# The seam between out_proj and the up projection: weight buffers of the second and third pair exchanged, GpSimd's low parts and weight sums earlier, the last norm ahead of part of the operand sums

## The chip, the cores and the metric

One core of a Trainium2 chip runs the whole program, a decoder layer in fp32. The metric is the device time of one execution in microseconds, taken as the median of three runs. The engines are named as in the profile: PE is the matrix engine (TensorE), DVE is VectorE, ACT is ScalarE, POOL is GpSimd, and SP is the engine that issues most of the DMAs. Times are microseconds from the start of the span unless marked otherwise.

## The reference, cut to what matters

The layer has a mixing part (recurrence, attention and cross-attention, merged by gates) and a convolutional feed-forward part. The change lies where the first ends and the second begins:

```python
x = x + merged @ w_out[l]                 # out_proj
x = x + conv_ffn(x, norm2_g[l], w_up[l], conv_w[l], conv_b[l], w_down[l])

def conv_ffn(x, g, w_up, conv_w, conv_b, w_down):
    h = rms_norm(x, g) @ w_up             # 1024 x 1024 by 1024 x 5632
    acc = conv_b + hp[:, 0:t] * conv_w[0] + hp[:, 1:t+1] * conv_w[1] + hp[:, 2:t+2] * conv_w[2]
    gate, val = jnp.split(acc, 2, axis=-1)
    return (jax.nn.silu(gate) * val) @ w_down
```

Here `hp` is `h` with two rows of zeros ahead. The sequence and the model width are 1024, and `w_up` gives 2 x 2816 columns.

## The kernel before, in words

**Precision.** PE multiplies in fp32r. Each fp32 operand is split into a high part (ACT copies it to fp32r) and a low part (the operand minus the high part, on DVE or POOL). A product is three matmuls: high by high, high by low, low by high. So every operand of PE costs one ACT row and one DVE or POOL row before PE can use it.

**Out_proj and its norms.** `mm` multiplies a block of 128 tokens (tt = 0 to 7) by `w_out`. `norm(tt)` is a generator with two stops: it adds the residual to the two halves (L1346, DVE) and squares them with sums (ACT); it forms the reciprocal root (L1350, L179, and a small step of POOL on L180); then ACT scales the row (L1353). `spread(tt)` turns the scaled block over with eight transposes on PE (L105) and writes them into the operands `raw0`, `raw1` (L1368 on ACT, L1370 on DVE). The first seven blocks are done inside out_proj. Block 7 is left to the up projection: `up_phase` receives its norm as a generator and its spread as a function.

**The up projection.** `up_phase` works on 22 pairs of 128-column blocks of `w_up`. A pair is a 2 x 2 block product done with seven products instead of eight. Each product has 12 matmuls of 512 columns. Its operands on the token side are the blocks "11", "21", "22" and the sums T1 to T4; on the weight side they are the pair's raw blocks `w1`, `w2` and the sums of them. The token sums are the subtractions of `sums` (L1377); half 0 of it makes T1 and T2, half 1 the two others. `old` is tokens 0 to 383 of each half of the tokens, `new` is tokens 384 to 511, which only exist once block 7 is through its norm. `split_hi` (L1390, ACT) and `split_lo` (L1395, DVE, or POOL for "22") split the token operands.

**Weights of a pair.** `load(n)` fetches them (L1478). `prep1` splits `w1`. `prep2` forms two sums on POOL (`it`, L1504 and L1505) and splits them (L1482 on ACT, L1485 on POOL). `prep3` forms two differences on POOL (L1517 writes `w2`, L1518 writes `s4`) and splits them. Even pairs lie in the buffers `rw`, odd ones in `wr`. Pair 0's weights, and the first block of pair 1, are split earlier, in out_proj (`self.early`). The two buffers of `wr` hold the token sums t2 until the last `sums` and splits of T2 are through.

**Steps.** `step(n, i)` issues product i of pair n and the DVE or ACT rows that read its bank: step 6 adds p1 to the bank (L1607), and product 7 then goes on in the same bank, so PE waits for that DVE row; step 7 forms the second output `v` from the bank and from C (L1616, L1617), and product 3 goes on in bank C after that; step 4 subtracts D (L1626); step 3 closes the first output (L1633). `conv` applies the convolution: a start value on ACT (g, L1551), two DVE rows per half (L1552, L1553), then the gate (L1556, L1557 or L1562). `act_sums` forms four sums of the gated values for the down projection (L1570, gall) and sends them out.

**What sets the order.** A scheduler orders each engine's rows, except where a row is pinned: `self.pinned` and `keep_in_program_order` hold a row to its place in the program on its engine. PE's matmuls, the token operands and the first pairs' rows are pinned. On all engines but PE a row that waits holds the rows behind it.

The order around the seam is written out by hand in `up_phase` (from L1649 on), up to the loop over the pairs.

## Time and profile before

| | us |
|---|---|
| median of three runs | 1789.2 (1789.01, 1789.2, 1790.83) |
| the profiled execution | 1789.81 |
| its span | 1788.0 |

The span is the time between the first and the last instruction of the profiled execution. The rest of its time lies around it. The granted PE clock is 0.999 in the mean over the span.

A row of a timeline gives the start, the duration, the engine, the line, the operation, the output and inputs by their names, the shape and how many instructions it groups; a bracket gives the idle time of the engine just before and what ended it. For PE the same bracket is a wait of the matmuls themselves. In a view of waits, a row gives the waiting engine and line, what it waited for, and the total, the number of times and the longest. A row of the windows view gives the stretch, its length, the busy time and the number of rows of each engine, the granted clock as a share of full speed, the busy share of the DMA engines and GB/s. This is the chain of the page's fourth part, followed back from the last instruction, by engine:

```profile
PE 84%; DVE 4%; POOL 2%; ACT 1%; DMA 1%; issue 1%; DVEq 0%; SPq 0%; POOLq 0%; ACTq 0%
```

Most of the chain is PE. The costliest groups of the page are these (busy and mean of one instruction, then the idle time of the engine ahead of them and what ended most of it):

```profile
L119 PE MATMUL mm<-BT,l 128*128 128x512 f32 x504 | 117.9, 389 | 1.4 <-POOL l L1485 1.4
L119 PE MATMUL mm<-BT,wh 128*128 128x512 f32 x352 | 108.7, 389 | 0.9 <-DVE BT L1395 0.9
L1485 POOL TENSOR_TENSOR l<-it,l 128x1024 fp32r<-128x1024 f32 x21 | 50.8, 2419 | 90.2 <-ACT l L1482 90.2
```

The 504 matmuls that read the split weight sums waited 1.4 us in all, once; POOL, which makes the low parts, waited 90.2 us for ACT's high parts, which cost nothing as long as PE had other work.

### The profile page before, as it was taken

To read this page: it belongs to the slowest core of one execution; us is meant where nothing else is said; L and a number is where in the kernel's file an instruction comes from. 1 tells how busy PE (TensorE), PEld (TensorE's weight loads), DVE (VectorE), ACT (ScalarE), POOL (GpSimd) and SP (SyncE) were. 2 spreads that over 40 slices of the span, in tenths; PEclk is the share of its full clock that TensorE was granted. 3 is DMA by queue.
4 is the path that set the end of the run, shared out by engine and by line. 5 is a ranking of instruction groups with operands and counts; after the bars stand their busy time and mean duration, and the time that the engine had idled before them with its cause. 6 is when DMAs were issued, how large, how long until landed. Compare 5 with 4: busy or idle time off the path is not lost.

```text
span 1788.0 us, 27326 instructions
## 1 busy us (share of the span) xinstructions
PE 1774.1 (99%) x10479; PEld 1443.4 (81%) x10479; DVE 1178.8 (66%) x1604; ACT 863.6 (48%) x1566; POOL 794.3 (44%) x448
## 2 busy tenths in 40 slices
PE   9999999999999999999999999999999999999999
PEld 6777778888888888777777888877888888888887
DVE  5667774898988624234444962687767777795596
ACT  6544343556666635534444334544444445454443
POOL 3223352332331453122332542487777677545454
PEclk9999999999999999999999999999999999999999
DMA  5155565111112343567654553223323323396476
GB/s 210 59 162 180 183 224 159 51 54 57 54 57 77 125 120 96 207 227 278 208 190 177 197 191 108 104 95 106 112 89 98 121 89 122 126 321 216 146 239 208
DMA packets 122771, 261.28 MB, mean 146 GB/s; under 512 B 28681, under 2 KB 43657, under 8 KB 122514
## 3 DMA queue, kind: packets, MB, share of 16 engines
q1 hardware_dynamic: 85026, 193.83, 32.9%
q10 hardware_dynamic: 33840, 53.10, 8.1%
q0 software_dynamic: 3776, 12.62, 2.3%
q8 instruction: 82, 1.34, 0.3%
q14 instruction: 47, 0.39, 0.1%
HBM read 178.99 MB, written 80.48 MB: 145 GB/s over the span
## 4 chain that ended last, share of the span: by engine, by line
PE 84%; DVE 4%; POOL 2%; ACT 1%; DMA 1%; issue 1%; DVEq 0%; SPq 0%; POOLq 0%; ACTq 0%
PE mm L119 68%; PE g L119 12%; PE g L105 4%; DMA A<-yd 1%; POOL wl L1485 0%; DVE gall L1570 0%; DVE it L554 0%; DMA ggd<-qk 0%; DVE inst L556 0%; DVE qk L472 0%; POOL l L1485 0%; DVE w L832 0%; DMA x<-in_x_dram 0%; POOL it L1505 0%; DVE at L520 0%
## 5 line engine op out<-in xcount | busy, mean ns | idle before, releaser
L81 POOL TENSOR_TENSOR wl<-wr,wh 128x1024 fp32r<-128x1024 f32 (+2 forms) x78 | 199.2, 2554 | 469.6 <-ACT wh L80 469.6
L119 PE MATMUL mm<-xhi,wh 128*128 128x512 f32 x784 | 260.1, 412 | 1.0 <-ACT xhi L207 0.4
L119 PE MATMUL mm<-xlo,wh 128*128 128x512 f32 x784 | 243.4, 392 | 0.0
L119 PE MATMUL mm<-xhi,wl 128*128 128x512 f32 x784 | 242.5, 391 | 0.2 <-POOL wl L81 0.2
L119 PEld LDWEIGHTS mm<-xlo,wh 128*128 128x128 f32 x784 | 147.2, 188 | 33.1
L119 PEld LDWEIGHTS mm<-xhi,wl 128*128 128x128 f32 x784 | 146.9, 188 | 33.3 <-POOL wl L81 1.0
L119 PEld LDWEIGHTS mm<-xhi,wh 128*128 128x128 f32 x784 | 136.5, 189 | 29.3 <-issue 6.1
L80 ACT ACTIVATE wh<-wr 128x1024 fp32r<-128x1024 f32 (+2 forms) x78 | 81.8, 1049 | 131.1 <-PE mm L119 100.0
L119 PE MATMUL mm<-dw,da 128*128 128x512 f32 x528 | 120.3, 389 | 0.0
L119 PE MATMUL mm<-BT,l 128*128 128x512 f32 x504 | 117.9, 389 | 1.4 <-POOL l L1485 1.4
L1774 POOL TENSOR_TENSOR dw<-draw,dw 128x512 fp32r<-128x512 f32 x55 | 82.4, 1506 | 76.0 <-ACT dw L1772 72.2
L119 PEld LDWEIGHTS mm<-dw,da 128*128 128x128 f32 x528 | 99.1, 188 | 20.6
L119 PEld LDWEIGHTS mm<-BT,l 128*128 128x128 f32 x504 | 94.5, 188 | 21.4 <-POOL l L1485 1.8
L119 PE MATMUL mm<-BT,wh 128*128 128x512 f32 x352 | 108.7, 389 | 0.9 <-DVE BT L1395 0.9
L937 DVE TENSOR_TENSOR_SCAN at<-at,nrt 128x128 f32<-128x128 f32 (+3 forms) x64 | 96.4, 1514 | 19.5 <-ACT at L931 19.3
L119 PE MATMUL mm<-B,wh 128*128 128x512 f32 x352 | 108.5, 389 | 0.0
L1773 DVE TENSOR_TENSOR da<-draw,da 128x512 fp32r<-128x512 f32 x77 | 64.7, 846 | 51.3 <-ACT da L1771 49.4
L1485 POOL TENSOR_TENSOR l<-it,l 128x1024 fp32r<-128x1024 f32 x21 | 50.8, 2419 | 90.2 <-ACT l L1482 90.2
L119 PE MATMUL g<-dw,da 128*128 128x512 f32 x396 | 90.2, 389 | 0.0
L119 PEld LDWEIGHTS g<-dw,da 128*128 128x128 f32 x396 | 74.3, 188 | 15.4
L1771 ACT ACTIVATE da<-draw 128x512 fp32r<-128x512 f32 x77 | 48.1, 627 | 79.4 <-PE mm L119 32.2
L832 DVE TENSOR_TENSOR w<-w,nrt 128x1024 f32<-128x1024 f32 x24 | 46.6, 1940 | 57.3 <-ACT w L831 49.5
(337 smaller groups left out, 3980.3 us busy)
## 6 DMA issues: line engine op xcount, KB each, us to landing
wr<-in_w_in_dram SPq DMA_DIRECT2D x48, 512.0 KB, 3.6
draw<-actd SPq DMA_DIRECT2D x77, 256.0 KB, 3.4
draw<-in_w_down_dram SPq DMA_DIRECT2D x55, 256.0 KB, 4.4
at<-scr SPq DMA_DIRECT2D x24, 512.0 KB, 5.9
wr<-in_w_up_dram SPq DMA_DIRECT2D x22, 512.0 KB, 3.5
actd<-gall ACTq DMA_DIRECT2D x44, 256.0 KB, 3.0
rw<-in_w_up_dram SPq DMA_DIRECT2D x20, 512.0 KB, 3.6
gsd<-w ACTq DMA_DIRECT2D x18, 512.0 KB, 3.0
```

What stands on the lines that cost most here:

```text
L80: (fix_hi or fix)(self.nc.scalar.activation(hi, raw, AF.Copy))
L81: fix(self.nc.gpsimd.tensor_tensor(lo, raw, hi.bitcast(F32), ALU.subtract))
L105: self.pinned(self.nc.tensor.transpose(out, in_, self.ident[:n, :n]))
L119: self.pinned(self.nc.tensor.matmul(*a, **k))
L832: fix(nc.vector.tensor_tensor(g, g, self.nrb, ALU.mult))
L937: self.pinned(nc.vector.tensor_tensor_scan(sn[:, :W][:, ::-1], sn[:, :W][:, ::-1], self.nrt[:, 1152 - W :][:, ::-1], 1.0, ALU.mult, ALU.max))
L1485: ins = nc.gpsimd.tensor_tensor(lo, src, hi.bitcast(F32), ALU.subtract)
L1771: self.pinned(nc.scalar.activation(A[:, 0], a, AF.Copy))
L1773: self.pinned(nc.vector.tensor_tensor(A[:, 1], a, A[:, 0].bitcast(F32), ALU.subtract))
L1774: nc.gpsimd.tensor_tensor(Wt[:, 1], w, Wt[:, 0].bitcast(F32), ALU.subtract)
```

## The change

**Buffers.** `load` puts pairs 0, 2, 4 and so on into `wr` and the odd ones into `rw`. Pair 1's weights so no longer need t2's buffers, and are asked for (pinned on SP) right after the first stop of norm 7; the x of block 7 is asked for ahead of them, where it stood between the two loads of pair 2 before. Pair 2's weights now need t2's buffers.

**POOL.** The two sums of pair 1's weights become a function of their own (`weight_sums`) that is called right behind the norm's reciprocal root. The low parts of "22" stand ahead of that root. For pairs 1 and 2 the rows of `prep2` and `prep3` are pinned on POOL.

**DVE.** Half 1 of `sums(256, 384)` leaves out_proj. Its two parts (j = 0, 1) stand behind norm 7's residual adds, one ahead of the reciprocal root and one behind it. The last act_sums of pair 1 are split in two: two rows in step 6 of pair 2, two behind step 7's rows.

**ACT.** T2's second high part stands behind the norm's scaling; T1's second high part is done in one piece. T3's parts are split j by j, and pair 0's last weights are split ahead of T3's high parts.

The first of three places is POOL at the seam. Before (B is the low part of "22", `ss` the norm's small step, `it` the sums of pair 1's weights, `wl<-wsec` and `l<-wsum` low parts of pair 0's weights, `l<-it` that of pair 1's sums):

```order
L81 TENSOR_TENSOR wl_10501<-qk_10498,wh_10500 128x1024
L180 TENSOR_TENSOR ss_1592_10534<-rs_10542,half 128x1
L1395 TENSOR_TENSOR B_1_0_10511<-A_9821,B_0_0_10509 128x2x384
L1395 TENSOR_TENSOR B_1_1_10512<-A_9822,B_0_1_10510 128x2x384
L1485 TENSOR_TENSOR wl_10648<-wsec_10307,wh_10647 128x1024
L1395 TENSOR_TENSOR B_1_0_10511<-A_9821,B_0_0_10509 128x2x128
L1395 TENSOR_TENSOR B_1_1_10512<-A_9822,B_0_1_10510 128x2x128
L1504 TENSOR_TENSOR it_10690<-wr_10612 128x512
L1505 TENSOR_TENSOR it_10690<-it_10690,wr_10611 128x512
L1485 TENSOR_TENSOR l_1607_10674<-wsum_10308,l_1606_10673 128x512
L1485 TENSOR_TENSOR l_1611_10694<-it_10690,l_1610_10693 128x1024
```

and of the change:

```order
L81 TENSOR_TENSOR wl_10497<-qk_10494,wh_10496 128x1024
L1395 TENSOR_TENSOR B_1_0_10507<-A_9821,B_0_0_10505 128x2x384
L1395 TENSOR_TENSOR B_1_1_10508<-A_9822,B_0_1_10506 128x2x384
L180 TENSOR_TENSOR ss_1592_10528<-rs_10544,half 128x1
L1502 TENSOR_TENSOR it_10547<-rw_10535 128x512
L1503 TENSOR_TENSOR it_10547<-it_10547,rw_10534 128x512
L1487 TENSOR_TENSOR wl_10633<-wsec_10307,wh_10632 128x1024
```

The two low parts have moved ahead of the norm's step, and pair 1's sums follow it at once, where they stood behind four other rows.

The second place is DVE around norm 7's adds (`raw`, `A` and `t` are the token operands and sums, `x` the residual, `ss` and `rs` the norm, BT the low parts of T1 and T2). Before:

```order
L1377 TENSOR_TENSOR t_1522_9824<-A_9822,raw_9818 128x2x128
L1377 TENSOR_TENSOR A_9819<-A_9821,A_9819 128x2x128
L1377 TENSOR_TENSOR raw_9818<-t_1521_9823,raw_9818 128x2x128
L1377 TENSOR_TENSOR A_9820<-A_9822,A_9820 128x2x128
L1377 TENSOR_TENSOR raw_9818<-t_1522_9824,raw_9818 128x2x128
L1346 TENSOR_TENSOR x_1591_10531<-mm_10422,x_1591_10531 128x512
L1346 TENSOR_TENSOR x_1591_10531<-mm_10423,x_1591_10531 128x512
L1395 TENSOR_TENSOR BT_1_0_10515<-raw_9818,BT_0_0_10513 128x2x384
L1350 TENSOR_TENSOR ss_1592_10534<-ss_1592_10534 128x1
L179 TENSOR_SCALAR rs_10542<-ss_1592_10534 128x1
```

and of the change:

```order
L1377 TENSOR_TENSOR t_1522_9824<-A_9822,raw_9818 128x2x128
L1346 TENSOR_TENSOR x_1591_10525<-mm_10422,x_1591_10525 128x512
L1346 TENSOR_TENSOR x_1591_10525<-mm_10423,x_1591_10525 128x512
L1377 TENSOR_TENSOR A_9819<-A_9821,A_9819 128x2x128
L1377 TENSOR_TENSOR raw_9818<-t_1521_9823,raw_9818 128x2x128
L1350 TENSOR_TENSOR ss_1592_10528<-ss_1592_10528 128x1
L179 TENSOR_SCALAR rs_10544<-ss_1592_10528 128x1
L1377 TENSOR_TENSOR A_9820<-A_9822,A_9820 128x2x128
L1377 TENSOR_TENSOR raw_9818<-t_1522_9824,raw_9818 128x2x128
L1395 TENSOR_TENSOR BT_1_0_10511<-raw_9818,BT_0_0_10509 128x2x384
```

Four sums have moved behind the adds, two of them behind the reciprocal root, and T1's low part follows them.

The third place is POOL at pair 2's weights (`it` are their sums, L1517 and L1518, or L1522 and L1523, the differences, `l<-it` the low part of the sums, the second `wl` the low part of the differences). Before:

```order
L1485 TENSOR_TENSOR wl_10795<-rw_10762,wh_10794 128x1024
L1504 TENSOR_TENSOR it_10860<-rw_10763 128x512
L1505 TENSOR_TENSOR it_10860<-it_10860,rw_10762 128x512
L1517 TENSOR_TENSOR rw_10763<-rw_10762,rw_10763 128x512
L1518 TENSOR_TENSOR s_1646_10916<-rw_10762,it_10860 128x512
L1485 TENSOR_TENSOR l_1639_10864<-it_10860,l_1638_10863 128x1024
L1485 TENSOR_TENSOR wl_10920<-rw_10763,wh_10919 128x1024
```

and of the change:

```order
L1487 TENSOR_TENSOR wl_10794<-wr_10761,wh_10793 128x1024
L1502 TENSOR_TENSOR it_10859<-wr_10762 128x512
L1503 TENSOR_TENSOR it_10859<-it_10859,wr_10761 128x512
L1487 TENSOR_TENSOR l_1639_10863<-it_10859,l_1638_10862 128x1024
L1522 TENSOR_TENSOR wr_10762<-wr_10761,wr_10762 128x512
L1523 TENSOR_TENSOR s_1646_10915<-wr_10761,it_10859 128x512
```

The low part of the sums has moved ahead of the two differences. ACT's rows there keep their order: the high part of the sums, the high part of the differences (wh), and then the start values g of pair 1's convolution.

The diff:

```diff
--- before.py
+++ after.py
@@ -1372,11 +1372,11 @@
         def halves(j):
             return [raw0[:, 2 * j : 2 * j + 2], raw0[:, 4 + 2 * j : 6 + 2 * j], raw1[j], raw1[2 + j]]
 
-        def sums(t0, t1, which=(0, 1)):
+        def sums(t0, t1, which=(0, 1), js=(0, 1)):
             ts = slice(t0, t1)
             sub = lambda o, x, y: self.pinned(nc.vector.tensor_tensor(o, x, y, ALU.subtract))
             for half in which:
-                for j in range(2):
+                for j in js:
                     b11, b21, b12, b22 = (x[:, :, ts] for x in halves(j))
                     if half == 0:
                         sub(b11, b12, b11)
@@ -1410,7 +1410,7 @@
             elif tt == 5:
                 sums(0, 256)
             elif tt == 6:
-                sums(256, 384)
+                sums(256, 384, (0,))
 
         self.B, sqs = {}, {}
         t2 = [self.pool_wt.tile([128, 2, 512], F32, name=self.nm("t2"), tag="wr", bufs=2) for _ in range(2)]
@@ -1471,11 +1471,13 @@
 
         def load(n):
             if n < len(pairs):
-                tag, m = ("rw", pairs[n][0]) if n % 2 == 0 else ("wr", pairs[n][0])
-                pool = self.pool_r if n % 2 == 0 else self.pool_wt
+                tag, m = ("wr", pairs[n][0]) if n % 2 == 0 else ("rw", pairs[n][0])
+                pool = self.pool_wt if n % 2 == 0 else self.pool_r
                 W[n] = [pool.tile([128, 1024], F32, name=self.nm(tag), tag=tag, bufs=2) for _ in range(2)]
                 for i in range(2):
-                    nc.sync.dma_start(W[n][i], self.I["w_up"][m + i])
+                    ins = nc.sync.dma_start(W[n][i], self.I["w_up"][m + i])
+                    if n == 1:
+                        self.pinned(ins)
 
         def hl(src, pool, tags, n=1024, keep=False, queue=False):
             hi, lo = (pool.tile([128, n], F32R, name=self.nm(t), tag=t, bufs=16 if t == "l4" else 2) for t in tags)
@@ -1493,17 +1495,20 @@
             w = self.early[4 * n] if n < 2 else hl(W[n][0], self.pool_wt, ("wh", "wl"), keep=n == 2, queue=n == 2)
             st[n, 1], st[n, 2] = [[x[:, c] for x in w] for c in (L, R)]
 
+        def weight_sums(n):
+            w1, w2 = W[n]
+            s = st[n, "s"] = self.t4("it")
+            fix = self.tc.keep_in_program_order if n < 3 else lambda ins: ins
+            fix(nc.gpsimd.tensor_tensor(s[:, L], w2[:, L], w2[:, R], ALU.add))
+            fix(nc.gpsimd.tensor_tensor(s[:, R], s[:, L], w1[:, L], ALU.subtract))
+
         def prep2(n):
             if n == 0:
                 w = self.early[1]
             else:
-                w1, w2 = W[n]
-                s = self.t4("it")
-                st[n, "s"] = s
-                fix = self.tc.keep_in_program_order if n == 2 else lambda ins: ins
-                fix(nc.gpsimd.tensor_tensor(s[:, L], w2[:, L], w2[:, R], ALU.add))
-                fix(nc.gpsimd.tensor_tensor(s[:, R], s[:, L], w1[:, L], ALU.subtract))
-                w = hl(s, self.pool_l, ("l4", "l4"))
+                if n > 1:
+                    weight_sums(n)
+                w = hl(st[n, "s"], self.pool_l, ("l4", "l4"), keep=n == 1, queue=n < 3)
             st[n, 5], st[n, 6] = [[x[:, c] for x in w] for c in (L, R)]
 
         def prep3(n):
@@ -1513,10 +1518,10 @@
                 w1, w2 = W.pop(n)
                 s = st.pop((n, "s"))
                 s4 = self.pool_r.tile([128, 512], F32, name=self.nm("s4"), tag="s4", bufs=1)
-                fix = self.tc.keep_in_program_order if n == 1 else lambda ins: ins
+                fix = self.tc.keep_in_program_order if n < 3 else lambda ins: ins
                 fix(nc.gpsimd.tensor_tensor(w2[:, L], w1[:, L], w2[:, L], ALU.subtract))
                 fix(nc.gpsimd.tensor_tensor(s4, w1[:, R], s[:, R], ALU.subtract))
-            w = hl(w2, self.pool_wt, ("wh", "wl"), keep=n == 1, queue=n == 1)
+            w = hl(w2, self.pool_wt, ("wh", "wl"), keep=n < 2, queue=n < 2)
             st[n, 7], st[n, 4] = [[x[:, c] for x in w] for c in (L, R)]
             if n == 1:
                 return s4
@@ -1606,15 +1611,16 @@
                     st[n, "u1"] = u_tile()
                 self.pinned(nc.vector.tensor_tensor(st[n, "u1"][:, R2], Bk, st[n, "p1"], ALU.add))
                 if n and pairs[n - 1][2]:
-                    if n == 2:
-                        act_sums(pairs[n - 1][1], False)
-                    act_sums(pairs[n - 1][1], True)
+                    act_sums(pairs[n - 1][1], n > 2)
             elif i == 7:
                 Bk = st.pop((n, "B"))
                 product(n, 7, Bk, False, True)
                 v = st[n, "u2"] = u_tile()
                 nc.vector.tensor_tensor(v[:, L2], Bk, st.pop((n, "p1")), ALU.add)
-                nc.vector.tensor_tensor(v[:, R2], st[n, "C"], v[:, L2], ALU.add)
+                ins = nc.vector.tensor_tensor(v[:, R2], st[n, "C"], v[:, L2], ALU.add)
+                if n == 2:
+                    self.pinned(ins)
+                    act_sums(pairs[n - 1][1], True)
             elif i == 40:
                 Dk = st[n, "D"] = bank()
                 product(n, 4, Dk, True, True)
@@ -1653,42 +1659,48 @@
         prep1(1)
         hi("22", old)
         hi("T1", old, (0,))
-        hi("T2", old)
         next(norm)
+        load(1)
+        lo("22", old, eng=nc.gpsimd)
+        sums(256, 384, (1,), (0,))
+        hi("T2", old, (0,))
+        next(norm)
+        weight_sums(1)
+        sums(256, 384, (1,), (1,))
         lo("T1", old, (0,))
-        next(norm)
-        hi("T1", old, (1,))
-        lo("T2", old)
-        lo("22", old, eng=nc.gpsimd)
+        lo("T2", old, (0,))
         step(0, 1)
         evacuate(0)
         next(norm, None)
+        hi("T2", old, (1,))
+        lo("T2", old, (1,))
         st[1, "A"] = bank()
         product(1, 1, st[1, "A"], True, True)
         spread()
         evacuate(1)
         sums(384, 512, (0,))
-        hi("T1", new)
+        hi("T1", new, (0,))
+        hi("T1", js=(1,))
         lo("T1", new, (0,))
         lo("T1", js=(1,))
         hi("T2", new)
         lo("T2", new)
-        load(1)
         step(0, 2)
+        prep3(0)
         hi("T3", old)
         step(1, 2)
-        prep3(0)
         sums(384, 512, (1,))
-        lo("T3", old)
         hi("T3", new)
-        lo("T3", new)
+        for j in range(2):
+            for ts in (old, new):
+                lo("T3", ts, (j,))
         hi("22", new)
         lo("22", new, eng=nc.gpsimd)
         operand("T4", self.pool_a, "A", bufs=4)
         hi("T4")
         lo("T4")
         prep2(0)
-        st[0, 3] = hl(self.early[3][:, R], self.pool_l, ("l4", "l4"), 512, True)
+        st[0, 3] = hl(self.early[3][:, R], self.pool_l, ("l4", "l4"), 512, True, True)
         step(0, 5)
         prep2(1)
         step(0, 6)
```

## The prediction

> **What bounds the kernel now.** I read the page first, for the share of each engine.
>
> ```profile
> span 1788.0 us, 27326 instructions
> PE 1774.1 (99%) x10479; PEld 1443.4 (81%) x10479; DVE 1178.8 (66%) x1604; ACT 863.6 (48%) x1566; POOL 794.3 (44%) x448
> ```
>
> TensorE works 1774.1 of 1788.0 us, and the change leaves its instructions and their order as they are. The time can therefore move only by TensorE's waits and by its clock. All edits lie in the seam and in the first three pairs behind it, so the second view is PE's waits from 1141 to 1260 us (total, times, longest), and the third the PE timeline there.
>
> ```profile
> PE mm L119 <- DVE u L1617: 2.3, 1, 2.3
> PE mm L119 <- POOL l L1485: 1.4, 1, 1.4
> PE mm L119 <- DVE BT L1395: 0.9, 1, 0.9
> PE g L105 <- ACT sq L1353: 0.7, 1, 0.7
> PE mm L119 <- ACT l L1482: 0.4, 1, 0.4
> ...
> 1145.62 0.61 PE L119 MATMUL mm<-it,mg 128*128 128x512 f32 x2
> ...
> 1152.42 1.09 PE L105 MATMUL g<-kon,sq 128*128 128x128 f32 x8 [0.75 <-ACT sq L1353]
> ...
> 1171.48 0.70 PE L119 MATMUL mm<-B,l 128*128 128x512 f32 x2 [0.41 <-ACT l L1482]
> ...
> 1192.67 1.20 PE L119 MATMUL mm<-BT,l 128*128 128x512 f32 x4 [1.41 <-POOL l L1485]
> ...
> 1200.51 0.62 PE L119 MATMUL mm<-BT,wh 128*128 128x512 f32 x2
> ...
> 1208.38 4.58 PE L119 MATMUL mm<-B,l 128*128 128x512 f32 x12 [2.27 <-DVE u L1617]
> ```
>
> Five waits, 5.7 us in all. The last one has a tail: its 12 matmuls take 4.58 us. The view by windows says why.
>
> ```profile
> core 0: us, PE busy (x) PEld busy (x) DVE busy (x) ACT busy (x) POOL busy (x), PEclk, DMA share, GB/s
> 1188.00:1198.00 10.00, 8.59 (x38) 6.80 (x37) 7.14 (x11) 5.99 (x9) 9.92 (x7) 1.00 0.47 155
> 1209.30:1212.72 3.42, 3.42 (x10) 2.65 (x9) 2.78 (x4) 1.96 (x3) 3.42 (x2) 0.50 0.06 8
> 1212.72:1230.00 17.28, 17.28 (x77) 14.31 (x77) 8.69 (x15) 7.53 (x11) 11.52 (x8) 1.00 0.20 60
> ```
>
> Right behind the wait of 2.27 us the granted clock is 0.50 for 3.42 us, so about 1.7 us of work is lost. The wait of 1.41 us (in the first stretch) left the clock at 1.00. Waits and clock give a ceiling of 7.4 us for any gain here.
>
> The fourth reading is how VectorE and GpSimd hinder each other, because the change puts GpSimd's work beside VectorE's.
>
> ```profile
> L1570 DVE TENSOR_TENSOR gall<-gall x44: 677/1723/2878, 1200.0 to 1589.3; 128x512 f32<-128x512 f32 x44
> ...
> L1505 POOL TENSOR_TENSOR it<-it,wr x11: 1287/1295/2156, 1168.2 to 1530.6; 128x512 f32<-128x512 f32 x11
> ...
> 1200.02 6.88 DVE L1570 TENSOR_TENSOR gall<-gall 128x512 f32<-128x512 f32 x4
> ...
> 1201.82 2.84 POOL L1485 TENSOR_TENSOR l<-it,l 128x1024 fp32r<-128x1024 f32 x1
> ...
> 1185.40 0.69 DVE L1616 TENSOR_TENSOR u<-mm,p 128x512 f32<-128x512 f32 x1 [3.32 <-PE mm L119]
> ...
> 1185.12 1.29 POOL L1504 TENSOR_TENSOR it<-rw 128x512 f32<-128x512 f32 x1
> ```
>
> A VectorE sum with both inputs in SBUF takes 0.677 us at best and 1.723 in the median: four of them took 6.88 us beside GpSimd. GpSimd's row of the same size goes from 1.287 to 2.156. A VectorE row with one input in PSUM (L1616, 0.69) ran at full speed beside a GpSimd row of 1.29. I read this as taking turns: a VectorE row with two SBUF inputs waits for GpSimd's running row to end, and the other way round. The Trainium skill, "GPSIMD Engine Reference", section "1. Specifications", says that GpSimd shares its SBUF interfaces with VectorE, with contention for DVE instructions with two SBUF inputs. The rows agree; the rule speaks against the half of this change that puts GpSimd's rows between VectorE's operand sums, and without it the first term below would be negative (third rival).
>
> **First term: the seam, +2.5 us.**
>
> ```profile
> 1141.81 2.40 POOL L81 TENSOR_TENSOR wl<-qk,wh 128x1024 fp32r<-128x1024 f32 x1 [2.21 <-ACT wh L80]
> ...
> 1150.05 1.13 POOL L180 TENSOR_TENSOR ss<-rs,half 128x1 f32<-128x1 f32 x1 [5.84 <-DVE rs L179]
> ...
> 1144.91 0.85 ACT L1390 ACTIVATE B<-A 128x768 fp32r<-128x768 f32 x1 [0.92 <-PE mm L119]
> ...
> 1151.22 1.15 ACT L1353 ACTIVATE sq<-x,ss 128x1024 f32<-128x1024 f32 x1 [0.55 <-POOL ss L180]
> ...
> 1145.42 0.41 DVE L1377 TENSOR_TENSOR A<-A,A 128x256 f32<-128x256 f32 x1
> ...
> 1147.39 1.29 DVE L1346 TENSOR_TENSOR x<-mm,x 128x512 f32<-128x512 f32 x2 [0.55 <-DMA x<-in_x_dram]
> ...
> 1153.78 1.13 DVE L1370 TENSOR_SCALAR A<-g,params 128x128 f32<-128x128 f32 x4 [2.14 <-ACT A L1368]
> ...
> 1170.64 0.69 DVE L1699 TENSOR_TENSOR u<-mm,u 128x512 f32<-128x512 f32 x1
> ```
>
> Before, GpSimd is idle for 5.84 us between its low part of qk (ends 1144.21) and the norm's small step, so the sums run undisturbed and the residual adds (L1346) start at 1147.39, after 0.55 us for their x. Now x is asked for ahead of the weights, so that wait goes, and four sums of 0.41 us fewer stand in front. But the two low parts of "22" now stand on GpSimd ahead of the norm. Each is three quarters of a 2.40 us row, about 1.8. By turns: first sum to 1144.5, low part to 1146.2, second sum to 1146.5, low part (its high part is ready at 1145.76) to 1148.2, two sums to 1148.8. The adds start about 1.4 later. GpSimd's small step lost most of its 1.13 us to VectorE's operand rows, and those are shorter now, so I let 0.8 of the 1.4 reach ACT's scaling: it ends near 1153.2 instead of 1152.37, and PE's transposes wait 0.8 longer.
>
> Behind that, VectorE's list before its evacuations (L1370) holds two more sums, and its last low part of T2 needs an ACT high part that now stands behind the scaling (to about 1154.0). GpSimd's two sums for pair 1 (1.29 each) start near 1152.0 and alternate with those low parts (about 0.9 each): 1152.0 + 1.29 + 0.9 + 1.29 + 0.9 = 1156.3. The evacuations start at 1156.3 against 1153.78, 2.5 later. From there to L1699, which ends at 1171.33, VectorE's rows follow each other with no idle before any, and PE started at 1171.48: no slack. So PE is 2.5 late there, and this takes in the 0.8 above. Ends: -2.0 (the adds go first and the waits of 0.7, 0.9 and 0.4 all go) and +3.2 (the 0.8 adds to it). I take 2.5, the walk along the rows.
>
> The earlier loading of pair 1 ends a wait of GpSimd, not of PE, and is costed at nothing: VectorE's list hides it. The transfers themselves are the same ones; pair 2's now wait for t2's slots, which come free over 15 us before pair 2's first use. Ends: nothing and 0.4, the PE wait on ACT's l.
>
> **Second term: pair 2's low part, -1.0 us.**
>
> ```profile
> 1186.48 1.30 POOL L1505 TENSOR_TENSOR it<-it,rw 128x512 f32<-128x512 f32 x1
> 1187.74 1.29 POOL L1517 TENSOR_TENSOR rw<-rw,rw 128x512 f32<-128x512 f32 x1
> ...
> 1190.25 2.37 POOL L1485 TENSOR_TENSOR l<-it,l 128x1024 fp32r<-128x1024 f32 x1
> ...
> 1187.81 1.06 ACT L1482 ACTIVATE l<-it 128x1024 fp32r<-128x1024 f32 x1 [5.42 <-POOL it L1505]
> 1189.06 1.06 ACT L1482 ACTIVATE wh<-rw 128x1024 fp32r<-128x1024 f32 x1 [0.19 <-POOL rw L1517]
> 1190.03 1.47 ACT L1551 ACTIVATE g<-u,params 128x512 f32<-128x512 f32 x2
> ...
> 1190.83 1.46 DVE L1552 SCALAR_TENSOR_TENSOR g<-u,params,g 128x512 f32<-128x512 f32 x2 [3.29 <-ACT g L1551]
> ...
> 1199.41 0.69 DVE L1607 TENSOR_TENSOR u<-mm,p 128x512 f32<-128x512 f32 x1
> ```
>
> The low part of the sums starts at 1190.25, behind the two differences; its high part was ready at 1188.87. Put first, it is 1.38 earlier, and PE's wait for it was 1.41. I take -1.0; ends -1.4 and -0.4.
>
> **Third term: what that pushes back, +4.2 us.** Count from the end of the sums (1187.78). Before: ACT's high part of them beside GpSimd's first difference, then ACT's wh, and the gate's g starts 2.25 us after the sums. Now the first difference waits for the low part, and ACT's queue holds g behind wh, which needs the difference: 1.06 + 2.37 + 1.29 + 1.06 = 5.78. That is 3.5 later. VectorE's chain starts with that g and runs without a gap to L1607, which ends at 1200.10 and frees the bank for product 7 of pair 2 (PE 1200.51). With the seam's 2.5 it ends at 1206.1 and PE goes on at about 1206.2. PE arrives at 1200.51 + 2.5 - 1.0 = 1202.0. The new wait is 4.2; ends 2.5 (part of the chain is made up) and 5.0.
>
> **Fourth term: the split of the sums of gall, -2.3 us.** Only two of the four rows now stand ahead of L1616 and L1617, and a product of T4 without a wait lies between; the wait of 2.27 goes. Ends -2.3 and -1.3.
>
> **Rest, +0.5 us.** The other two rows of gall (median 1.723 each) now stand ahead of the subtraction that feeds pair 2's gate. That reaches PE at pair 3, if at all: ends 0 and 1.2, and I choose near the middle.
>
> **Clock, 0.** A wait of 2.27 us was followed by 3.42 us at 0.50, so one of 4.2 will be: 1.7 lost before, 1.7 after. The Trainium skill, "TensorE: Matmul & The Clock Gate", part 1, has the clock halved only after at least one idle window of about 3.4 us. The trace's 2.27 differs from it. By that rule too the new wait would halve the clock, but one under 3.4 us would not, which would take 1.7 us off the first rival. Ends of the term: -1.7 and +1.7.
>
> **Sum.** 2.5 - 1.0 + 4.2 - 2.3 + 0.5 = **+3.9**. The profiled execution took 1789.8 us (span 1788.0), so 1793.7. It stands 0.6 above the median of the three runs, 1789.2: I forecast **1793.1 us**.
>
> **The rivals.** A measurement of this kernel can tell about 0.2%, 3.6 us.
> - *The pushback is partly made up.* The seam costs 1.0 only and the new wait 2.5: 1.0 - 1.2 + 2.5 - 2.3 + 0.5 = +0.5, 1789.7. For it: PE's waits hide part of any delay. Against: no idle row in VectorE's chain. 0.20.
> - *A second half-clock stretch.* A wait of 1.5 at the transposes or one of 4.2 could halve the clock twice: +5.6, 1794.8. For it: 2.27 sufficed. Against: 1.41 did not. 0.10.
> - *The other side: VectorE goes first at the seam.* If its sums are not made to take turns with the low parts, the adds start once out_proj's last matmul (1145.62, in the PE rows above) is done at 1146.23, a microsecond before 1147.39, and three waits go: -2.0. Then pair 2: VectorE's chain -2.0 + 3.5 = +1.5 at product 7, then -2.3 and +0.5: -0.3, 1788.9. It decides if the adds start before 1147.4. Against: the 6.88 us row. 0.11.
> - *Faster outright.* If ACT's g is not held behind wh, the third term is 0, and with it the half clock may go: from 2.5 - 1.0 - 2.3 - 1.7 = -2.5 to -7.4: 1781.8 to 1786.7, most of it under 1785.6. It needs wh to end within 2.3 us of the sums. Against: wh needs the difference, and ACT keeps its order. 0.09.
>
> **How the numbers follow.** Forecast 0.50, own range 1791.3 to 1795.3; of it 0.34 is above 1792.8 (slower by over 0.2%) and 0.16 below. Slower: 0.34 + 0.10 = 0.44. Within 0.2%: 0.16 + 0.20 + 0.11 = 0.47. Faster: 0.09. The range leaves out the last rival and half of the second: 1787.0 to 1795.6.
>
> **What would show it.** Right: the transposes of the last norm about 0.8 later; evacuations (L1370) near 1156.3; PE near 1174 where it was 1171.48; wh of pair 2 starting some 4.7 us after its sums; a PE wait of about 4.2 on VectorE's L1607 (now L1612) ahead of product 7; no wait on L1617; 0.50 clock after it. Wrong: adds before 1147.4, or g of pair 1 within 3 us of pair 2's sums.

## The result, and the profile after

| | median, us | range, us | runs |
|---|---|---|---|
| before | 1789.46 | 1788.5 to 1790.83 | 9 |
| with the change | 1794.87 | 1793.66 to 1795.34 | 9 |

The ratio is 1.0029, with a 95% interval of 1.0020 to 1.0037: the change costs 5.4 us, or 0.3%, and the interval lies wholly above 1. The forecast was 1793.1 in a range of 1787.0 to 1795.6.

The profiled execution took 1793.66 us. This is its page, and the view of PE's waits from 1141 to 1260 us (total, times, longest):

```profile
span 1791.9 us, 27324 instructions
...
PE 1774.8 (99%) x10479; PEld 1442.7 (81%) x10479; DVE 1186.9 (66%) x1604; ACT 863.4 (48%) x1565; POOL 794.8 (44%) x448
```

```profile
PE mm L119 <- DVE u L1612: 4.3, 1, 4.3
PE mm L119 <- DVE BT L1395: 2.0, 2, 1.6
PE g L105 <- ACT sq L1353: 1.5, 1, 1.5
PE mm L119 <- DVE u L1711: 0.8, 1, 0.8
PE mm L119 <- POOL l L1487: 0.2, 1, 0.2
```

PE does the same work in nearly the same time (1774.8 against 1774.1), and waits more. The wait of 2.3 us on L1617 is gone, and that of 1.4 us on POOL's low part is down to 0.2. In their place stands one of 4.3 us on L1612, which is L1607 of before. The two executions reach the seam at slightly different times, so a stage is compared by what it adds. The row to start from is DVE's evacuation of block 6, ahead of all that the change moves. First before, then with the change:

```profile
1142.63 1.13 DVE L1370 TENSOR_SCALAR A<-g,params 128x128 f32<-128x128 f32 x4 [3.66 <-ACT A L1368]
```

```profile
1142.37 1.13 DVE L1370 TENSOR_SCALAR A<-g,params 128x128 f32<-128x128 f32 x4 [3.66 <-ACT A L1368]
...
1152.95 1.09 PE L105 MATMUL g<-kon,sq 128*128 128x128 f32 x8 [1.54 <-ACT sq L1353]
...
1174.29 2.96 PE L119 MATMUL mm<-B,l 128*128 128x512 f32 x12 [0.78 <-DVE u L1711]
...
1194.23 5.29 PE L119 MATMUL mm<-BT,l 128*128 128x512 f32 x22 [0.20 <-POOL l L1487]
...
1206.54 1.22 PE L119 MATMUL mm<-BT,wh 128*128 128x512 f32 x2 [4.31 <-DVE u L1612]
...
1213.54 2.88 PE L119 MATMUL mm<-B,l 128*128 128x512 f32 x12
1216.26 0.61 PE L119 MATMUL mm<-B,wh 128*128 128x512 f32 x2
```

The changed kernel arrives 0.26 us early. Its rows stand against 1171.48, 1192.67, 1200.51 and 1208.38 of before, and with the 0.26 added back PE is late by 3.07, 1.82, 6.29 and 5.42 us. The last of these is two things at once. The 24 matmuls from product 7 up to there take 5.44 us at full clock (12 of them lie between 1213.54 and 1216.26, so 0.227 each). Before they took 7.87, with the wait of 2.43 by this count; now they take 7.00, without a wait, because the clock was halved. The windows view shows it:

```profile
core 0: us, PE busy (x) PEld busy (x) DVE busy (x) ACT busy (x) POOL busy (x), PEclk, DMA share, GB/s
...
1206.50:1210.00 3.50, 3.46 (x9) 2.78 (x10) 3.46 (x2) 0.00 (x0) 3.34 (x3) 0.56 0.01 2
```

The mean of 0.56 holds the end of the stretch, which is over by about 1209.6. The half-clock stretch costs 1.56 us here, and the one of before is gone: the 12 matmuls behind it take 2.88 instead of 4.58.

| stage | forecast, us | measured, us |
|---|---|---|
| seam | +2.5 | +3.07 |
| pair 2's low part | -1.0 | -1.25 |
| wait ahead of product 7 | +4.2 | +4.47 |
| wait on L1617 | -2.3 | -2.43 |
| half clock | 0 | +1.56 - 1.70 |
| rest, up to the end of the span | +0.5 | +0.4 |
| sum | +3.9 | +4.1 |

The rest arises where the prediction looked for it, at pair 3. The other two rows of gall (3.55 us from 1212.36) stand ahead of the subtraction (L1632, 1215.83), and PE starts pair 3's product 7 at 1227.39, as soon as its L1612 row ends (1226.65 and 0.69). Before, PE started there at 1223.69 without waiting for that row. No run takes these two rows of gall out by themselves, so this is read from the rows alone.

The spans differ by 3.9 us (the 4.1 less the early arrival), the medians by 5.4. The profiled execution is the lowest of the nine; the last section comes back to that.

**The seam.** DVE and POOL take turns where the change put POOL's low parts (B) beside the operand sums (raw, t):

```profile
1143.41 2.82 DVE L1377 TENSOR_TENSOR raw<-A,raw 128x256 f32<-128x256 f32 x2
1146.15 2.40 DVE L1377 TENSOR_TENSOR t<-A,raw 128x256 f32<-128x256 f32 x2
1148.47 1.27 DVE L1346 TENSOR_TENSOR x<-mm,x 128x512 f32<-128x512 f32 x2
...
1152.43 4.00 DVE L1395 TENSOR_TENSOR BT<-t,BT 128x768 fp32r<-128x768 f32 x2
1156.36 1.11 DVE L1370 TENSOR_SCALAR A<-g,params 128x128 f32<-128x128 f32 x4
...
1143.90 4.03 POOL L1395 TENSOR_TENSOR B<-A,B 128x768 fp32r<-128x768 f32 x2
...
1151.69 1.96 POOL L1502 TENSOR_TENSOR it<-rw 128x512 f32<-128x512 f32 x1
1153.73 1.89 POOL L1503 TENSOR_TENSOR it<-it,rw 128x512 f32<-128x512 f32 x1
```

Four sums of 0.41 us take 5.2 us. The residual adds (L1346) start at 1148.47 without waiting for their x, 1.3 us later than before by the same count. Behind the norm, pair 1's weight sums, which stood behind five more rows of POOL before, take turns with T2's low parts (1.82 us before, 4.00 now), and the last evacuations start 2.84 us later than before (1156.36 against 1153.78, and the 0.26).

**Pair 2.** ACT, POOL and DVE from pair 2's weight sums on:

```profile
1190.64 1.06 ACT L1484 ACTIVATE l<-it 128x1024 fp32r<-128x1024 f32 x1 [5.44 <-POOL it L1503]
1195.45 1.06 ACT L1484 ACTIVATE wh<-wr 128x1024 fp32r<-128x1024 f32 x1 [3.75 <-POOL wr L1522]
1196.42 1.47 ACT L1556 ACTIVATE g<-u,params 128x512 f32<-128x512 f32 x2
...
1191.78 2.39 POOL L1487 TENSOR_TENSOR l<-it,l 128x1024 fp32r<-128x1024 f32 x1 [1.17 <-ACT l L1484]
1194.13 1.29 POOL L1522 TENSOR_TENSOR wr<-wr,wr 128x512 f32<-128x512 f32 x1
...
1197.22 1.46 DVE L1557 SCALAR_TENSOR_TENSOR g<-u,params,g 128x512 f32<-128x512 f32 x2 [6.90 <-ACT g L1556]
...
1205.80 0.69 DVE L1612 TENSOR_TENSOR u<-mm,p 128x512 f32<-128x512 f32 x1
```

ACT waits 3.75 us for the difference (L1522) that stands behind POOL's low part, and g stands behind ACT's wh: it starts 5.78 us after ACT's high part of the sums does (1190.64 to 1196.42), where it was 2.22 before (1187.81 to 1190.03). DVE has waited 6.90 us for that g when it starts. Nothing is made up on the way to L1612, which ends at 1206.49.

### The profile page after: what moved, and what is told of

It is laid out like the page before. It is cut to its first block, busy times and chain, and to the rows that moved or that the text cites. A ratio compares the mean times of both kernels' runs of the same rounds, so it can differ in the third digit from the quotient of the medians.

```text
span 1791.9 us, 27324 instructions
## 1 busy us (share of the span) xinstructions
PE 1774.8 (99%) x10479; PEld 1442.7 (81%) x10479; DVE 1186.9 (66%) x1604; ACT 863.4 (48%) x1565; POOL 794.8 (44%) x448
## 4 chain that ended last, share of the span: by engine, by line
PE 84%; DVE 4%; issue 1%; POOL 1%; ACT 1%; DMA 1%; DVEq 0%; SPq 0%; ACTq 0%; POOLq 0%
PE mm L119 68%; PE g L119 12%; PE g L105 4%; DMA A<-yd 1%; POOL l L1487 0%; DVE BT L1395 0%; DVE raw L1377 0%; DMA scr<-at 0%; DVE it L554 0%; DVE inst L556 0%; DVE w L832 0%; POOL wl L1487 0%; DVE qk L472 0%; POOL hf L779 0%; ACT BT L1390 0%
## 5 line engine op out<-in xcount | busy, mean ns | idle before, releaser
L1556 ACT ACTIVATE g<-u,params 128x512 f32<-128x512 f32 x88 | 65.1, 770 | 44.8 <-DVE u L1639 23.9
```

Of the source, the lines that this page charges most:

```text
L1556: nc.scalar.activation(c, u[:, 2 + h * 512 : 514 + h * 512], AF.Identity, scale=self.par("cw2", m), bias=self.par("cb", m))
```

## The experiments

Ten kernels were run in three sittings, each with the kernel before beside them (medians 1790.06, 1790.26 and 1789.86). Two theories stood at the start. **A, the queue:** the 4.3 us come from the order on POOL and ACT at pair 2. **B, the seam:** they are the seam's 3 us, handed on by DVE.

| run | median, us | ratio to before, 95% interval |
|---|---|---|
| pair 2's order as before | 1793.91 | 1.0022 (1.0013 to 1.0031) |
| seam as before | 1792.86 | 1.0018 (1.0009 to 1.0027) |
| before, with the split of gall alone | 1790.60 | 1.0003 (0.9994 to 1.0012) |
| low parts of 22 back | 1793.55 | 1.0020 (1.0011 to 1.0030) |
| g ahead of wh | 1795.88 | 1.0030 (1.0019 to 1.0041) |
| that, and pair 3's low part earlier | 1791.74 | 1.0008 (0.9999 to 1.0016) |
| before, mended | 1786.92 | 0.9981 (0.9972 to 0.9990) |
| low parts of 22 and pair 1's sums back | 1793.99 | 1.0022 (1.0013 to 1.0030) |
| those, and the operand sums back | 1793.14 | 1.0019 (1.0010 to 1.0028) |
| seam as before, mended | 1788.98 | 0.9998 (0.9989 to 1.0006) |

**Pair 2's order as before.** The first line is in `prep2`, the second in `prep3`.

```diff
-    w = hl(st[n, "s"], self.pool_l, ("l4", "l4"), keep=n == 1, queue=n < 3)
+    w = hl(st[n, "s"], self.pool_l, ("l4", "l4"), keep=n == 1, queue=n < 2)
...
-    fix = self.tc.keep_in_program_order if n < 3 else lambda ins: ins
+    fix = self.tc.keep_in_program_order if n < 2 else lambda ins: ins
```

> The change with one part undone: at pair 2 GpSimd forms the two differences ahead of the low part of the sums again, as before. Theory A (the queue): the wait of 4.3 us on L1612 ahead of product 7 comes from this order alone, since ACT's wh and behind it pair 1's g wait for the difference. Then that wait falls under 0.5 us, g starts some 3.5 us earlier against pair 2's sums, PE's wait for pair 2's low part is back at 1.2 to 1.8 us, and the half-clock stretch behind it goes (1.5 us). A further wait of up to 2.5 us can open behind, at pair 3's first weights, whose low part GpSimd makes after pair 4's sums. Time 1790.0 to 1793.0, against 1794.9. Theory B (the seam): the 4.3 us are the seam's delay of 3 us handed on by VectorE; then the wait stays above 3 us and the time within 1 us of 1794.9.

PE's waits in this kernel (the three left out are 0.8 to 1.9 us in all each, on DVE and ACT, and stand at the seam):

```profile
PE mm L119 <- POOL wl L1487: 2.5, 1, 2.5
...
PE mm L119 <- POOL l L1487: 1.4, 1, 1.4
...
```

The wait on L1612 is gone from the list, and pair 2's 1.4 us are back: theory A holds for it, and B falls. But the time is 1793.91, 0.9 over what A expected. The wait of 2.5 us on POOL's low part of pair 3's first weights is the one that was thought possible; not expected was a half-clock stretch behind it (0.55 from 1216.0 to 1219.5).

**Seam as before.** Everything between the first token high part and `step(0, 5)` is taken from the kernel before, with all sums in `late(6)` and pair 1's weight sums in `prep2`.

> The change with the seam put back to the order of before (low parts of 22 behind the root, all operand sums in out_proj, pair 1's weight sums late); buffers, pair 2's order and the split of gall stay. Theory A: PE's delay at the seam (3.1 us) goes but the wait ahead of product 7 stays at 4.0 to 4.8 us with its half clock: 1791.3 to 1792.3. Theory B: without the seam's delay that wait falls under 1.5 us: 1788 to 1789.5.

The wait ahead of product 7 is 4.31 us, as in the change, with the seam's delay all but gone (table below): B falls a second time. The time is 0.6 over the range. In this trace the same wait drew two half-clock stretches in a row, which cost 2.7 us instead of 1.56, and the recorded clocks (last section) tell of two in 8 of the 11 executions. The three with one have a median of 1792.10, inside the range.

**Before, with the split of gall alone.** This asks whether the wait on L1617 was worth its 2.3 us.

```diff
-                    if n == 2:
-                        act_sums(pairs[n - 1][1], False)
-                    act_sums(pairs[n - 1][1], True)
+                    act_sums(pairs[n - 1][1], n > 2)
...
+                if n == 2:
+                    self.pinned(ins)
+                    act_sums(pairs[n - 1][1], True)
```

> The kernel before with the split of the four gall sums alone. If the wait of 2.27 us on L1617 and the half clock behind it (1.7 us) are all there is, both go: 1789.5 - 4.0 = 1785.5. The rival (a covered wait): GpSimd makes pair 4's sums and difference ahead of pair 3's low part (its rows from 1204.73 on), which is done near 1211.6; PE without its wait on L1617 gets there near 1209.5, so a wait of 2.0 to 2.5 us on GpSimd's L1485 opens at pair 3's first product, with a half-clock stretch of its own: 1788.5 to 1789.7, no gain.

```profile
1212.06 0.50 PE L119 MATMUL mm<-B,wl 128*128 128x512 f32 x1 [2.51 <-POOL wl L1485]
...
1207.94 1.75 POOL L1517 TENSOR_TENSOR rw<-rw,rw 128x512 f32<-128x512 f32 x1
1209.65 2.35 POOL L1485 TENSOR_TENSOR wl<-wr,wh 128x1024 fp32r<-128x1024 f32 x1
```

The wait on L1617 is gone, and 3.3 us of matmuls later PE waits 2.51 us for POOL, which made pair 4's sum (`it`) and difference (`rw`) ahead of pair 3's low part (`wl`). 1790.60 against 1790.06 is no difference: the rival holds, and the wait of before had covered another of the same size. The time is 0.9 over the rival's range. Its half clock did not come in the profiled execution, but by the recorded clocks (last section) it came in 8 of the 11; these have a median of 1790.78, the three without one of 1789.47.

**Low parts of 22 back behind the norm's root.**

```diff
-        lo("22", old, eng=nc.gpsimd)
         sums(256, 384, (1,), (0,))
         hi("T2", old, (0,))
         next(norm)
+        lo("22", old, eng=nc.gpsimd)
         weight_sums(1)
```

> The change with the two low parts of 22 on GpSimd put back behind the norm's reciprocal root; all else as in the change. If VectorE and GpSimd take turns on rows with two SBUF inputs, the residual adds start when out_proj's last matmul is done (2 us earlier than in the change), and PE's wait for the norm falls from 1.5 to under 0.5 us. If GpSimd's rows are not what holds VectorE there, the adds stay where they are in the change. The delay of PE at pair 0's last product is only partly cured (by 0 to 1.0 us), since the same rows then stand beside the low parts of T1 and T2; the wait ahead of product 7 stays at 4.0 to 4.8. Time 1793.5 to 1795.

```profile
1146.38 1.29 DVE L1346 TENSOR_TENSOR x<-mm,x 128x512 f32<-128x512 f32 x2 [0.54 <-PE mm L119]
...
1159.53 0.50 PE L119 MATMUL mm<-BT,wsh 128*128 128x512 f32 x1 [0.96 <-DVE BT L1395]
```

The adds now wait only for out_proj's last matmul, 2.7 us earlier than in the change by the same count, and PE's wait for the norm is gone. POOL's two rows were what held DVE there. PE's delay at pair 0's last product falls by 0.5 only: a new wait of 0.96 us, for a low part of DVE, opens at 1159.53.

**Low parts of 22 and pair 1's weight sums back; then the operand sums too.** The first adds to the edit above that `weight_sums(1)` goes back into `prep2(1)`. The second:

```diff
-                sums(256, 384, (0,))
+                sums(256, 384)
...
-        sums(256, 384, (1,), (0,))
-        sums(256, 384, (1,), (1,))
```

> The change with both moves of GpSimd's rows at the seam undone: the low parts of 22 behind the reciprocal root, and pair 1's weight sums where they were, behind pair 0's low parts. By turns, the residual adds start at once after out_proj (2 us earlier than in the change), VectorE's evacuations (L1370) start 1.5 to 2.5 us earlier than in the change, and PE's wait for the norm falls under 0.5 us. PE's delay at pair 0's last product then falls from 3.1 by 0.5 to 1.5 us only, since the sums that were moved behind the adds, and pair 1's weight sums beside the low parts of T3 and T4, still stand in VectorE's list: 1793.0 to 1794.5. If the two moves are the whole cause at the seam, that delay falls under 0.5: 1791.5 to 1792.3.

> As the run with both moves of GpSimd's rows undone, and the half of the operand sums that the change moved behind the residual adds is back in out_proj, ahead of them. If the rest of the seam's delay comes from these sums standing in VectorE's list behind the norm, the evacuations (L1370) start 1.0 to 1.7 us earlier than in that run and PE's delay at pair 0's last product against the kernel before falls from 1.5 to between 0 and 0.5; the wait ahead of product 7 stays at 4.3. Time 1791.8 to 1793.2. If it comes from the order of T3's low parts or from the buffers, the delay stays over 1.2 and the time at 1793.5 to 1794.5.

PE's delay at pair 0's last product is the start of the PE row less 1171.48, less what the run was late at the first L1370 row (against 1142.63):

| | PE row | L1370 | delay, us |
|---|---|---|---|
| the change | 1174.29 | 1142.37 | 3.07 |
| low parts of 22 back | 1174.38 | 1142.95 | 2.58 |
| and pair 1's weight sums | 1173.38 | 1143.00 | 1.53 |
| and the operand sums | 1171.93 | 1142.53 | 0.55 |
| seam as before | 1172.41 | 1143.30 | 0.26 |

So the seam's 3.07 us, undone in this order and with one trace for each step, are 0.5 from the low parts, 1.05 from the weight sums, 1.0 from the operand sums moved behind the adds, and 0.5 from the rest. The last of the three runs is 0.05 over what its theory allowed, and the wait ahead of product 7 stays at 4.31 us in both.

**g ahead of wh.** The change with one edge on ACT: `start` is the second start value g of pair 1's first convolution in `conv_half`.

```diff
             ins = nc.scalar.activation(hi, src, AF.Copy)
+            if after is not None:
+                self.tc.add_manual_dep(ins.ins, after.ins.name, dep, reason="behind the start value")
...
+            if (n, i) == (1, 1):
+                self.start = ins
...
-            w = hl(w2, self.pool_wt, ("wh", "wl"), keep=n < 2, queue=n < 2)
+            w = hl(w2, self.pool_wt, ("wh", "wl"), keep=n < 2, queue=n < 2, after=self.start if n == 2 else None)
```

> The change with one edge added on ACT: wh of pair 2 stands behind the first two start values g of pair 1's convolution. GpSimd's order is that of the change. Theory A in its narrow form (g held behind wh in ACT's queue is what makes VectorE's chain late): g starts within 1.3 us of the end of ACT's high part of pair 2's sums, instead of 4.7 us, and the wait of 4.3 us on L1612 goes (under 0.5). What it covered comes out: PE then waits 4 to 5 us for GpSimd's low part of pair 3's first weights, since GpSimd's rows there are not a bit earlier; time 1793.5 to 1795. If the chain is late for another reason (the low part itself, or GpSimd's turns), the wait on L1612 stays above 3 us. If nothing stands behind it, the time falls to 1790.

```profile
1192.19 1.06 ACT L1484 ACTIVATE l<-it 128x1024 fp32r<-128x1024 f32 x1 [5.45 <-POOL it L1506]
1193.16 1.47 ACT L1559 ACTIVATE g<-u,params 128x512 f32<-128x512 f32 x2
...
1217.35 0.50 PE L119 MATMUL mm<-B,wl 128*128 128x512 f32 x1 [4.21 <-POOL wl L1490]
```

g starts right behind ACT's high part, and the wait on DVE is gone, with POOL's order up to the differences as in the change: what made it was ACT's queue, with g behind a row that waits for POOL. But 4.2 us come back as a wait for POOL's low part of pair 3's first weights. PE starts product 7 at 1203.72 and stops for it 9.4 us later. The time is 1795.88, 0.9 over the range; it is 5.6 over before in its sitting, where the change is 5.4 over, so nothing is gained.

**That, and pair 3's low part ahead of pair 4's sums.** Pair 3's low part (`prep1`) and pair 4's sums (`weight_sums`) are pinned on POOL in this order, and `gate`, the last sigmoid of pair 2's gates, stands ahead of the high part of pair 4's sums on ACT.

```diff
-            w = self.early[4 * n] if n < 2 else hl(W[n][0], self.pool_wt, ("wh", "wl"), keep=n == 2, queue=n == 2)
+            w = self.early[4 * n] if n < 2 else hl(W[n][0], self.pool_wt, ("wh", "wl"), keep=n == 2, queue=n in (2, 3))
...
-            fix = self.tc.keep_in_program_order if n < 3 else lambda ins: ins
+            fix = self.tc.keep_in_program_order if n < 3 or n == 4 else lambda ins: ins
...
-                w = hl(st[n, "s"], self.pool_l, ("l4", "l4"), keep=n == 1, queue=n < 3)
+                w = hl(st[n, "s"], self.pool_l, ("l4", "l4"), keep=n == 1, queue=n < 3, after=self.gate if n == 4 else None)
```

> As the run before (g ahead of wh), and GpSimd makes the low part of pair 3's first weights ahead of pair 4's sums, with ACT's gates of pair 2 ahead of the high part of those sums. If the order on GpSimd is what makes that low part late, the wait of 4 to 5 us on it falls to 0.3, and no wait over 1.5 us is left behind product 3 of pair 0; the seam's 3.1 us stay. 1790.0 to 1791.5, against 1794.9 for the change. If GpSimd's amount of work is the bound and not its order, a wait of 2 us or more opens within the next two pairs, and the time stays above 1792.

```profile
1223.41 0.73 PE L119 MATMUL mm<-BT,wh 128*128 128x512 f32 x2 [0.86 <-DVE u L1551]
...
1233.22 0.50 PE L119 MATMUL mm<-B,wl 128*128 128x512 f32 x1 [0.90 <-POOL wl L1490]
```

The largest wait behind the seam is 0.90 us, and 4.1 us of the run before are gone, the half clock behind the wait among them: the order of the rows, not POOL's amount of work, made that low part late. The edits on POOL and on ACT came together, so this run does not tell them apart. The median is 0.2 over the range.

**Before, mended; and seam as before, mended.** The first puts five edits on the kernel before: the split of gall, g ahead of wh, pair 2's low part between the two differences, pair 3's low part ahead of pair 4's sums with the gates ahead, and block 7's x ahead of pair 2's weights (pinned on SP). The second puts the mended order of the run above on the run with the seam as before, so it keeps the exchanged buffers.

> The kernel before with five edits: the split of gall, at pair 2 the low part of the sums between the two differences and g ahead of wh, at pair 3 the low part of the first weights ahead of pair 4's sums with the gates ahead, and the x of block 7 asked for ahead of pair 2's weights. By theory A with the covered waits all cured, PE's waits of 1.4 and 2.27 us fall to 0.6 and under 0.9, the norm's from 0.75 to 0.4, and no half-clock stretch is left: 1790.0 - 0.8 - 1.4 - 0.3 - 1.7 = 1785.8, range 1784.5 to 1787.5. If GpSimd's amount of work is the bound, a wait of 2 us or more opens later and the time stays at 1788.5 to 1790.

> The seam of the kernel before, the exchanged buffers, and the mended order of pairs 2 to 4 (g ahead of wh, pair 3's low part ahead of pair 4's sums). By theory A the wait ahead of product 7 is under 0.5, no wait is over 1.2, there is no half-clock stretch, and the time is the mended kernel of before plus the 0.3 to 1.0 us that the exchanged buffers and the pinned rows cost at pair 0's last and pair 1's first product: 1787.2 to 1788.2. If the exchange of the buffers were itself a gain, it would be under 1786.9.

PE's waits in the first, the longest four:

```profile
PE mm L119 <- DVE BT L1397: 0.9, 1, 0.9
PE mm L119 <- POOL wl L1494: 0.8, 1, 0.8
PE mm L119 <- DVE u L1556: 0.7, 1, 0.7
PE g L105 <- ACT sq L1355: 0.7, 1, 0.7
...
```

No wait is over 0.9 us, and the time is 1786.92, 3.3 us under the kernel before and clear of its interval: it beats both kernels. One edit earned nothing. The adds start 0.6 earlier with x there in time, but PE's wait for the norm stays at 0.7, and ACT shows why:

```profile
1146.90 1.28 DVE L1348 TENSOR_TENSOR x<-mm,x 128x512 f32<-128x512 f32 x2
...
1146.53 1.56 ACT L1392 ACTIVATE BT<-t 128x768 fp32r<-128x768 f32 x2
1148.00 0.28 ACT L1554 ACTIVATE u<-kon 128x2 f32<-128x2 f32 x2
1148.18 0.62 ACT L1349 ACTIVATE sq<-x 128x512 f32<-128x512 f32 x1
```

The squares stand behind T2's high parts and the zero columns in ACT's queue. The second mended kernel comes out at 1788.98, no different from before and 0.8 over its range. It differs from the first in more than one edit and was run in another sitting, so the 2.1 us between them (2.5 when each is taken against before in its own sitting) are not split; they give no sign that the exchange of the buffers is a gain.

## Why the prediction was right, and where it was off

**Seam (+2.5; 3.07).** The mechanism is shown: DVE and POOL take turns, and taking POOL's rows away moves the adds by 2.7 us. The walk was right to 0.1 us at PE's transposes (1.54 waited, 1.55 by the sum) and short by 0.3 at the evacuations (2.84 against 2.5). The other 0.3 arose behind them. What the prediction left without a price is the operand sums themselves: it notes two more of them in DVE's list ahead of the evacuations, and its sum leaves them out. Moved behind the adds, they cost 1.0 of the 3.07.

**Pair 2's low part (-1.0; -1.25).** Right; the size lies between the chosen value and its end of -1.4.

**The pushback (+4.2; +4.47).** Right in place, cause and size. The narrow cause, g behind wh in ACT's queue, was the prediction's; the run with g ahead of wh shows it. The prediction adds the seam both to DVE's chain and to PE's arrival, so it drops out of this wait, and the traces bear that out: the wait is 4.31 us in all five kernels that keep this order, with seam delays from 0.26 to 3.07.

**The split of gall (-2.3; -2.43), and the clock (0; -0.14).** Right as terms of this sum, since PE came so late that POOL was ready. But the rival "faster outright" keeps the 2.3 us with the pushback gone, as a gain that the split has of its own. That reading was wrong: with the split alone on the kernel before, 2.51 us of waiting for POOL took the place of 2.27. The rival fell on the same step. It gave 1781.8 to 1786.7 if g were not held behind wh; with g freed and nothing else, the kernel took 1795.88, since a wait of 4.2 us on POOL stood behind the one removed. The ceiling of 7.4 us still stands as a bound (the largest gain measured is 3.3), but a gain read from the sum of the waits counts covered waits as if they were free.

**The median.** Forecast as the profiled difference (+3.9) on the median of before, and 1.8 low. Of this, 0.3 is the median of before, 1789.46 over nine executions where the forecast had 1789.2. The recorded clocks (last section) bear on the rest. The clock term of 0 compares two executions with one half-clock stretch each. But the kernel before has none in 37 of 81 executions, and the change has at least one in all nine. Executions with one stretch have medians of 1794.58 in the change (seven of them) and 1790.4 before (44, from the other sittings). That is 4.1 apart, as by the stages. So the term holds for the profiled pair and was too small for the median: the prediction took it that the wait of 2.27 us always draws a stretch.

**Luck.** The sum came within 0.2 us of the 4.1 of the stages in part because errors cancel: the seam and the pushback were 0.8 short together, the other terms 0.6 over.

## What to carry to other kernels

Before counting a wait as a gain, ask of each other input of the waiting instruction when it is ready: the next-latest sets what is left, and here it took back all of 2.3 us and all of 4.2. A row moved ahead on one engine is paid by the rows that it passes, and by what stands behind a waiting row in another engine's queue; follow the moved-back rows to the next engine, not only the moved-ahead one. Waits that cover each other have to be removed together, in the order in which they appear.

## What the runs showed of the hardware that was not expected

**The half clock.** It comes in stretches of about 3.4 us, and the length of a wait does not settle whether one follows. Waits of 2.27 us (before) and 2.48 us (pair 2's order as before) were followed by one; the wait of 2.51 us (split of gall alone) was not: the clock stayed at 1.00 up to the wait's end, as here, and in the 4 us behind it.

```profile
1207.00:1212.00 5.00, 2.55 (x12) 1.77 (x10) 4.84 (x6) 2.83 (x4) 5.00 (x3) 1.00 0.54 210
```

The same wait of 4.31 us drew one stretch in the change and two in the run with the operand sums back:

```profile
1203.30:1206.70 3.40, 2.00 (x5) 1.61 (x6) 3.33 (x6) 1.35 (x2) 3.32 (x3) 0.50 0.20 77
1206.70:1210.10 3.40, 3.40 (x10) 2.63 (x9) 1.62 (x2) 0.00 (x0) 3.32 (x3) 0.50 0.00 0
```

The first begins while PE still waits, and the two cost 2.7 us of matmul time. The Trainium skill, "TensorE: Matmul & The Clock Gate", part 1, tells of a free-running window of about 3.4 us, halved after at least one idle window. The length agrees, and a phase that runs free would explain one stretch here and two there; that a whole idle window is needed does not agree with the waits of 2.27 and 2.48. In the eight traces that have a stretch, it begins 2.2 to 4.9 us after the wait does.

Only one execution of each kernel has a trace, but every execution of the change and of the experiments' sittings has its mean granted clock on record, and that counts the stretches. In the twelve traces 1.000 goes with none, 0.999 with one and 0.998 with two, and the clock is full in the rest of the span. By this count the kernel before has one stretch in 44 of 81 executions (median 1790.4) and none in 37 (1789.3). Its wait of 2.27 us so draws a stretch in one execution and not in another. The change has one in seven of its nine executions and two in the other two (1795.17 and 1795.34). Its profiled execution has one, as have six that took 1794.07 to 1795.26, so the clock does not explain why it is the lowest of the nine; that stays open.

**Turns.** DVE rows of 0.41 us between POOL rows of about 2 us took 1.2 to 1.4 us each in the mean (2.82 and 2.40 for two). With POOL idle two of them took 0.75 (before, at 1144.75). That fits a price set by POOL's rows and not by DVE's, but no run varied the length of either.
